# A hybrid encoder layer on one core: another begin, earlier loads and sums, and 26 identity transposes in front of the first real one

## The chip, the core and the metric

The kernel runs on one core of a Trainium2 chip. The core has a matrix engine (PE, or TensorE; its weight loads are listed as PEld), a vector engine (DVE), a scalar engine (ACT), GpSimd (POOL), and SP, which here only issues transfers; 16 DMA engines move data between the chip's memory and the core's own memory (SBUF, and PSUM for the results of PE). The engines work through their own lists of instructions in order and wait for each other by semaphores. The metric is the device time of one execution in microseconds (us), the median of several.

## The reference

One layer of an encoder runs over two requests with the same weights: a sample of 512 tokens and a prompt of 1024, each behind 16 learned meta tokens. All is float32.

```
h = rmsnorm(x, g_mix)
z = h @ w_in                                 # q, k, v, u, gate_na, gate_fn
y_na = neighbourhood_attention(q, k, v, rel_bias, meta_bias) @ w_branch_na
y_fn = fourier_mix(u) @ w_branch_fn          # real part of a 2-D DFT
mixed = sigmoid(gate_na) * y_na + sigmoid(gate_fn) * y_fn
x = x + mixed @ w_out
a = relu(rmsnorm(x, g_mlp) @ w_up)
x = x + (a * a) @ w_down
```

D_MODEL is 1024, there are 8 heads of 64, and the MLP is 4096 wide. At the end stands another rmsnorm, and the meta tokens are dropped. Tokens attend to a neighbourhood of 8 rows by 16 columns of a 64-wide grid and to the meta tokens.

## The kernel before, in words

**Precision.** PE multiplies a rounded form of float32 ("fp32r" in the profile). Each operand is therefore split into a high part (a cast, by ACT, L155 for weights, L136 for results in PSUM) and a low part (the difference, by POOL or DVE, L157 or L137; L159 and L160 do the same with a scale). A product is three matmuls: hi x hi, hi x lo, lo x hi. `mm3` (the matmuls of L132) runs the first two kinds alternately over the 8 blocks of the 1024 rows, then the third. With `late="b"` (new in the diff's call) those that need the low part of the right operand, here the value weights, come last instead of those that need the low part of the left one. 24 matmuls of 128x512 make one block of results.

**The begin.** The sample comes first. `read` loads tokens (tile "xt", three buffers), normalizes them (L178 to L184: squares and root on ACT, reciprocal, refinement and the scaling into "hn" on DVE), and PE transposes 128x128 blocks against the identity (L194) into ps_t, from which "hT" is split. Meta rows come first, then the four tiles of 128 tokens. In between, four pieces of the value weights are loaded and split. `project_v` then multiplies: 24 matmuls for the meta rows and 24 for each tile. Behind that stand the weights of K and Q of the first pair of heads (`qk_weights`), the tables of the mask and biases (`tables`), and the attention, whose first matmuls have the lines L531 to L533.

**The attention of the sample.** For each unit of rows and heads a bias tile "bm" is loaded (L774 to L781), scores go to ps_s (L647, L648), the softmax runs on DVE and ACT (L652 to L656), the weights are transposed (L660) and multiplied with the values (L680). The values went through memory (vd, vf).

**Gates, folding, merge.** `gates` runs 16 steps, each of 24 matmuls, and lets other work advance between them by a list `beside` of generators with a first and a last step. One of these is `fold_u`: it loads a piece of w_in in transposed form and the channel DFT, multiplies them (L259) and stores the result "wu". `merge_na` multiplies attention's result with w_branch_na, whose blocks it loads into the tile "relu" (L825).

**Fourier, merge, projection.** `fourier_channels`, `fourier_positions` (with cosine and sine tables; `sines` loads a sine table from POOL's queue, L1030), `merge_fn`, then `project_out` with the weights "w_raw<-in_w_out" split into "wo_hi" and "wo_lo". It also loads x again into four tiles "acc" for the residual sum (L1091).

**The MLP.** `Up` does the sample's up projection while its generator `reading` normalizes the prompt's tokens beforehand (L184 into "r"). The prompt goes through the same stages, and its MLP is done in class `Halves` as a scheme of combined halves with fewer products: the weights of the down projection are first added up on DVE (L1642), then cast by ACT and split by POOL. The result of each block leaves PSUM by a sum on DVE (L1668), called an eviction below.

**What sets the order.** Each engine's list follows from the order in which the code is written, and a scheduler that brings instructions forward where their data allow. `behind(marks)` holds what is written inside it behind the instructions marked, and `pinned()` holds it behind the latest instruction of every engine. SP issues transfers in order, and a transfer into a tile waits for the tile's earlier users, so one that waits holds up all behind it.

Of the kernel before, what the change touches and what calls it, by code (L numbers as in the profile page):

```python
# [17 lines left out]
F32 = mybir.dt.float32  # L18
# [8 lines left out]
D = 1024  # L27
# [41 lines left out]
class Layer:  # L69
    def __init__(self, tc, ctx, ins, outs):  # L70
# [16 lines left out]
        nc.sync.dma_start(self.sgn, ins["sgn"])  # L87
        self.small = ctx.enter_context(tc.tile_pool(name="small", bufs=4))
        self.wpool = ctx.enter_context(tc.tile_pool(name="w", bufs=2))
        self.wv = {}  # L90
        self.meta_values = None
# [81 lines left out]
    def norm(self, x, gain, out, n=128, junk=None):  # L173
# [10 lines left out]
        nc.vector.scalar_tensor_tensor(out=out, in0=x, scalar=y, in1=gain[:n], op0=ALU.mult, op1=ALU.mult)  # L184
# [16 lines left out]
    def tables(self, marks):  # L201
# [15 lines left out]
        with self.behind(marks):  # L217
            nc.sync.dma_start(mask, self.ins["colmask"])
            nc.sync.dma_start(win, self.ins["rel_win"])
# [78 lines left out]

    def value_weights(self, q, to=None, lo_engine=None, raw="raw"):
        return self.weights(self.ins["w_in"][q * 256:(q + 1) * 256, VC:VC + 512].rearrange("(kt p) c -> p kt c", p=128), to,  # L300
                            lo_engine=lo_engine, raw=raw)

    def qk_weights(self, pr, to=(None, None)):
        return (self.weights(self.rows("w_in", KCOL + pr * 128), to[0], lo_engine=self.nc.vector if pr else None),
                self.weights(self.rows("w_in", QC + pr * 128), to[1], scale=-DH ** -0.5))

    def project_v(self, name, T, hT, p, wv):
# [12 lines left out]
        for t in range(-1 if meta is None else 0, T // 128):  # L320
# [3 lines left out]
            self.mm3(ps[:n, :], [(hT[0][:, kt, pos:pos + n], hT[1][:, kt, pos:pos + n],  # L324
                                  wv[kt // 2][0][:, kt % 2, :], wv[kt // 2][1][:, kt % 2, :]) for kt in range(8)])
            vs = p.tile([128, 512], F32R, name="pt0", tag="pt0", bufs=self.ptb).bitcast(F32)
            nc.vector.tensor_copy(vs[:n], ps[:n])
# [22 lines left out]
    def run(self, order):  # L350
# [6 lines left out]
        for i, (name, T) in enumerate(order):  # L357
# [5 lines left out]
            if i == 0:  # L363
                with pool("first", "right") as p:
                    gain = p.tile([128, D], F32, name="gain")
                    reading = self.read(name, T, hT, lambda: p.tile([128, D], F32, name="xt", bufs=3),
                                        lambda: p.tile([128, D], F32, name="hn", bufs=2), gain)
                    next(reading)
                    next(reading)
                    for q in range(4):  # L370
                        next(reading, None)
                        self.wv[q] = self.value_weights(q, self.pair(p, [128, 2, 512], bufs=4), self.nc.vector, ("raw", "raw", "hi", "lo")[q])
                    marks = self.mark((mybir.EngineType.SP,))
                    w0 = self.qk_weights(0)
# [1496 lines left out]
```

## Time and profile before

| | |
|---|---|
| runs of the kernel, median | 1923.19 us (1922.71 to 1925.18, 3 runs) |
| the profiled execution | 1927.61 us |
| its span | 1925.8 us |
| granted clock over the span | 0.998 |
| busy: PE, PEld | 1892.8 us (98%), 1588.0 us |
| busy: DVE, POOL, ACT | 1117.8 us, 816.5 us, 753.1 us |
| moved by DMA | 358.38 MB, 186 GB/s on average |

A line of the profile gives an instruction's line in the kernel, its engine, its operation and its tiles, written as out<-in with buffer numbers left out. "ps_mm", "ps_s", "ps_t" and "ps_o" are PSUM banks by their tags and are used in turn, so a name does not tell the stage; the time does. In a timeline row the two numbers ahead are start and duration in us; several instructions in a row are joined (x8), and brackets tell how long the engine had stood idle and what ended it. In the chain of work that ended last the numbers are start, length and what. In waits of an engine they are the sum in us, the number of times and the longest. A view by windows gives for each stretch its length, the busy time of each engine with its number of instructions in brackets, and then the clock granted to PE (1.00 is full speed), the busy share of the DMA engines, and GB/s.

### The profile page before, as it was taken

How to read it: one execution, taken by the hardware profiler on the slowest of the kernel's cores; microseconds unless marked ns; L12 is line 12 of the kernel's file. 1: busy time of each engine (PE TensorE's matmuls, PEld its weight loads, DVE VectorE, ACT ScalarE, POOL GpSimd, SP SyncE). 2: the span in 40 equal slices, each digit the busy share in tenths (PEclk: the TensorE clock that was granted, in tenths of full speed). 3: DMA queues.
4: the chain of work that ended last, by engine and by line, in shares of the span. 5: the costliest groups of instructions: out<-in, count | busy, mean ns of one | idle time of the engine just before them, and what ended most of it. 6: DMA issues, size and time to landing. Idle time of an engine off the chain costs nothing.

```text
span 1925.8 us, 26107 instructions
## 1 busy us (share of the span) xinstructions
PE 1892.8 (98%) x9435; PEld 1588.0 (82%) x9435; DVE 1117.8 (58%) x1749; ACT 753.1 (39%) x1351; POOL 816.5 (42%) x674
## 2 busy tenths in 40 slices
PE   7999999999999999999999999999999999999998
PEld 5888888888888888888898878888888888888886
DVE  5771554787625567660427376656665326758856
ACT  3674333443315556541223234333333333333434
POOL 1335543455422233342233218887882323323531
PEclk9999999999999999999999999999999999999999
DMA  6757873687756455463452523444446778567733
GB/s 221 192 152 236 232 218 124 208 271 251 237 191 173 121 145 156 120 233 105 117 158 85 175 99 121 158 173 164 173 155 250 269 250 285 207 218 281 277 118 127
DMA packets 312945, 358.38 MB, mean 186 GB/s; under 512 B 51768, under 2 KB 222392, under 8 KB 312264
## 3 DMA queue, kind: packets, MB, share of 16 engines
q1 hardware_dynamic: 295056, 334.93, 53.0%
q0 software_dynamic: 17760, 21.80, 5.0%
q8 instruction: 74, 1.21, 0.3%
q14 instruction: 55, 0.45, 0.1%
HBM read 263.06 MB, written 96.16 MB: 187 GB/s over the span
## 4 chain that ended last, share of the span: by engine, by line
PE 89%; DMA 4%; DVE 2%; issue 2%; POOL 1%; ACT 1%; SPq 0%; POOLq 0%; DVEq 0%; ACTq 0%
PE ps_mm L132 23%; PE ps_o L132 22%; PE ps_s L132 19%; PE ps_t L132 11%; PE ps_mm L531 3%; PE ps_mm L532 3%; PE ps_mm L533 3%; PE ps_o L680 2%; PE ps_t L660 1%; DMA relu<-in_w_na 1%; DMA bm<-g_un 1%; DMA sin<-in_sin_prompt 1%; PE ps_s L648 1%; PE ps_s L647 1%; PE ps_t L194 0%
## 5 line engine op out<-in xcount | busy, mean ns | idle before, releaser
L157 POOL TENSOR_TENSOR w_lo<-w_raw,w_hi 128x1024 fp32r<-128x1024 f32 x69 | 177.1, 2567 | 217.9 <-ACT w_hi L155 151.9
L157 POOL TENSOR_TENSOR w_lo<-raw,w_hi 128x1024 fp32r<-128x1024 f32 (+1 forms) x49 | 100.0, 2044 | 202.1 <-ACT w_hi L155 196.2
L155 ACT CAST w_hi<-w_raw 128x1024 fp32r<-128x1024 f32 x88 | 92.5, 1051 | 180.1 <-PE ps_s L132 58.5
L157 DVE TENSOR_TENSOR h_lo<-long,h_hi 128x1024 fp32r<-128x1024 f32 x54 | 77.1, 1428 | 94.1 <-ACT h_hi L155 94.1
L531 PE MATMUL ps_mm<-hT,w_hi 128*128 128x512 f32 (+2 forms) x296 | 121.5, 410 | 0.0
L532 PE MATMUL ps_mm<-hT,w_hi 128*128 128x512 f32 (+2 forms) x296 | 110.4, 373 | 0.0
L533 PE MATMUL ps_mm<-hT,w_lo 128*128 128x512 f32 (+2 forms) x296 | 110.4, 373 | 0.0
L155 ACT CAST h_hi<-long 128x1024 fp32r<-128x1024 f32 x54 | 56.7, 1050 | 101.6 <-PE ps_s L132 25.1
L654 ACT ACTIVATE sc<-sc,ast 128x288 f32<-128x288 f32 (+4 forms) x96 | 53.9, 561 | 68.3 <-DVE ast L652 68.0
L155 ACT CAST w_hi<-raw 128x1024 fp32r<-128x1024 f32 (+1 forms) x49 | 40.9, 840 | 100.9 <-DVE raw L1642 54.4
L157 DVE TENSOR_TENSOR hs_lo<-short,hs_hi 128x512 fp32r<-128x512 f32 x54 | 72.3, 1339 | 13.9 <-ACT hs_hi L155 11.7
L1421 POOL TENSOR_TENSOR x<-w_hi,x 128x512 fp32r<-128x512 f32 (+1 forms) x39 | 64.9, 1663 | 18.4 <-ACT x L1418 18.4
L680 PEld LDWEIGHTS ps_o<-pt,vb 104*64 104x64 f32 (+6 forms) x576 | 62.4, 163 | 9.7 <-POOL vb L617 2.6
L132 PE MATMUL ps_t<-gate,x 128*128 128x512 f32 x276 | 66.5, 390 | 0.0
L533 PEld LDWEIGHTS ps_mm<-hT,w_lo 128*128 128x128 f32 x296 | 55.7, 188 | 10.4
L680 PE MATMUL ps_o<-pt,vb 104*64 104x128 f32 (+6 forms) x576 | 62.1, 243 | 1.9 <-POOL vb L617 1.2
L617 POOL TENSOR_TENSOR vb<-vr,vb 96x384 fp32r<-96x384 f32 (+4 forms) x48 | 48.6, 1031 | 34.7 <-ACT vb L616 34.7
L132 PE MATMUL ps_mm<-gate,x 128*128 128x512 f32 x256 | 63.2, 389 | 0.0
L774 POOL MEMSET bm<- 64x96 f32 (+2 forms) x64 | 11.2, 175 | 117.1 <-DVE ast L652 101.7
L132 PEld LDWEIGHTS ps_t<-gate,x 128*128 128x128 f32 x276 | 51.7, 188 | 10.9 <-ACT w_hi L136 0.2
L652 DVE CUSTOM_DVE_ANT_0 sc<-ps_s,bm 128x288 f32<-128x288 f32 (+4 forms) x96 | 46.4, 483 | 23.6 <-issue 10.7
L532 PEld LDWEIGHTS ps_mm<-hT,w_hi 128*128 128x128 f32 x296 | 56.2, 190 | 1.6
(714 smaller groups left out, 5574.4 us busy)
## 6 DMA issues: line engine op xcount, KB each, us to landing
long<-hidden_prompt SPq DMA_DIRECT2D x54, 512.0 KB
w_raw<-in_w_in SPq DMA_DIRECT2D x52, 512.0 KB
raw<-in_w_down SPq DMA_DIRECT2D x39, 512.0 KB
w_raw<-in_w_up SPq DMA_DIRECT2D x34, 512.0 KB
hidden_prompt<-h SPq DMA_DIRECT2D x32, 512.0 KB
short<-hidden_sample SPq DMA_DIRECT2D x54, 256.0 KB
w_lo<-in_w_down SPq DMA_DIRECT2D x18, 512.0 KB
w_raw<-in_w_out SPq DMA_DIRECT2D x16, 512.0 KB
```

Source lines behind the costliest of these rows:

```text
L132: self.nc.tensor.matmul(out, a, b, start=(i == 0 and not more), stop=(i == len(terms) - 1), skip_group_check=more)
L155: nc.scalar.copy(out=hi, in_=raw)
L157: (lo_engine or nc.gpsimd).tensor_tensor(out=lo, in0=raw, in1=hi.bitcast(F32), op=ALU.subtract)
L531: nc.tensor.matmul(ps, a[0], b[0], start=(kt == 0), stop=False)
L532: nc.tensor.matmul(ps, a[0], b[1], start=False, stop=False)
L533: nc.tensor.matmul(ps, a[1], b[0], start=False, stop=(kt == 7))
L617: nc.gpsimd.tensor_tensor(out=lo, in0=vs, in1=hi.bitcast(F32), op=ALU.subtract)
L647: nc.tensor.matmul(ps[:, :W], qs[hh][:, qc], ks[hh][:, 0, kw[0], kw[1]], start=True, stop=False)
L652: nc.vector.tensor_tensor_reduce(out=sc[:, :W], in0=ps[:, :W], in1=bm[:, :W], scale=1.0, scalar=3e38, op0=ALU.add, op1=ALU.min, accum_out= ...
L654: nc.scalar.activation(out=sc[:, :W], in_=sc[:, :W], func=AF.Exp, bias=st[:, 0:1], scale=-1.0, accum_out=st[:, 1:2])
L680: nc.tensor.matmul(po[:m, j * 128:(j + 1) * 128], v, x, start=(i == 0), stop=(i == len(ops) - 1))
L1421: (engine or self.nc.gpsimd).tensor_tensor(out=w[1], in0=raw, in1=w[0].bitcast(F32), op=ALU.subtract)
```

## The change

It joins several edits.

- **Begin.** `read_first` replaces `read` for the sample. It loads x0, gain, w0, x1, w1, meta, w2, w3, x2, x3 in this order; x2 and x3 go into tiles "k" that the attention uses later. PE's list begins with 26 transposes of the identity into a PSUM bank that nothing reads. The first tile's last scaling is done in two halves of columns. Meta rows follow the third tile; their high and low parts are laid side by side in 48 columns, so that 16 matmuls do and a copy and a sum add up the result. The low part of K's weights is made by DVE instead of POOL. The small load "sgn" comes later.
- **Bias.** Six tiles bm are loaded ahead, before the last tile of the values is multiplied.
- **Folding.** `fold_u`'s loads are one step (0) and its matmuls the steps 2 to 9.
- **Residual.** The four loads of x into "acc" are issued behind the Fourier positions, pinned.
- **Reading.** The normalization of the prompt during the sample's `Up` is pinned.
- **Sines.** The second sine table of the prompt is loaded in two pieces of columns.
- **Sums.** In `Halves.down` the sums of weights for a coming step are given out between the evictions of the current one.

```diff
@@ norm
+        for i in range(parts):
+            cs = slice(i * D // parts, (i + 1) * D // parts)
+            nc.vector.scalar_tensor_tensor(out=out[:, cs], in0=x[:, cs], scalar=y, in1=gain[:n, cs], op0=ALU.mult, op1=ALU.mult)
@@ the new reading of the sample
+    def read_first(self, name, T, hT, gain, p, more):
+        nc = self.nc
+        xs, hns, raws = {}, {}, {}
+        def load(t):
+            n = NM if t < 0 else 128
+            xs[t] = p.tile([128, D], F32, name="xt", bufs=3) if t < 2 else more()
+            nc.sync.dma_start(xs[t][:n], self.ins["meta_tokens"] if t < 0 else self.ins[f"x_{name}"][t * 128:(t + 1) * 128, :])
+        def load_w(q):
+            raws[q] = self.wtile(("raw", "raw", "hi", "lo")[q], [128, 2, 512]).bitcast(F32)
+            nc.sync.dma_start(raws[q], self.value_rows(q))
+        def norm(t):
+            n = NM if t < 0 else 128
+            hns[t] = p.tile([128, D], F32, name="hn", bufs=2)
+            self.norm(xs[t][:n], gain, hns[t][:n], n, parts=1 if t else 2)
+        def turn(t):
+            self.transpose_in(hns[t], hT, 0 if t < 0 else self.lead + t * 128, NM if t < 0 else 128)
+        def split(q):
+            self.wv[q] = self.split_sb(raws[q], *self.pair(p, [128, 2, 512], bufs=4), lo_engine=nc.vector)
+        load(0)
+        self.gain(gain, "g_mix")
+        warm = self.psum("o")
+        for _ in range(26):
+            nc.tensor.transpose(warm[:, :128], self.ident, self.ident)
+        load_w(0)
+        load(1)
+        load_w(1)
+        load(-1)
+        load_w(2)
+        load_w(3)
+        for t in range(2, T // 128):
+            load(t)
+        norm(0)
+        split(0)
+        turn(0)
+        with self.behind(self.mark((mybir.EngineType.Activation, mybir.EngineType.DVE))):
+            norm(1)
+            split(1)
+            split(2)
+        turn(1)
+        split(3)
+        with self.behind(self.mark((mybir.EngineType.Activation, mybir.EngineType.DVE))):
+            norm(2)
+            turn(2)
+            for t in (-1, 3):
+                norm(t)
+                turn(t)
@@
+    def qk_weights(self, pr, to=(None, None), late=()):
+        return (self.weights(self.rows("w_in", KCOL + pr * 128), to[0], lo_engine=self.nc.vector if pr or late else None, lo_marks=late),
                 self.weights(self.rows("w_in", QC + pr * 128), to[1], scale=-DH ** -0.5))
@@ project_v
-        for t in range(-1 if meta is None else 0, T // 128):
+        order = list(range(T // 128))
+        for t in order if meta is not None else order[:-1] + [-1] + order[-1:]:
+            if meta is None and t == T // 128 - 1:
+                with self.behind(self.mark((mybir.EngineType.SP,))):
+                    self.first_bias(p, T)
             n = NM if t < 0 else 128
             pos = 0 if t < 0 else self.lead + t * 128
             ps = self.psum()
-            self.mm3(ps[:n, :], [(hT[0][:, kt, pos:pos + n], hT[1][:, kt, pos:pos + n],
-                                  wv[kt // 2][0][:, kt % 2, :], wv[kt // 2][1][:, kt % 2, :]) for kt in range(8)])
+            if t < 0:
+                own = p.tile([128, 512], F32R, name="pt1", tag="pt1", bufs=self.ptb)[:, :8 * 48].rearrange("p (k c) -> p k c", k=8)
+                nc.gpsimd.tensor_copy(own[:, :, NM:2 * NM].rearrange("p k (g c) -> p k g c", c=8),
+                                      self.zero[:, None, None, 0:8].to_broadcast([128, 8, 2, 8]))
+                for i in range(2):
+                    nc.scalar.copy(out=own[:, :, 32 * i:32 * i + NM], in_=hT[i][:, :, 0:NM].bitcast(F32))
+                for i in range(2):
+                    for kt in range(8):
+                        nc.tensor.matmul(ps[:48], own[:, kt], wv[kt // 2][i][:, kt % 2, :], start=(kt + i == 0), stop=(kt + i == 8))
+            else:
+                self.mm3(ps[:n, :], [(hT[0][:, kt, pos:pos + n], hT[1][:, kt, pos:pos + n],
+                                      wv[kt // 2][0][:, kt % 2, :], wv[kt // 2][1][:, kt % 2, :]) for kt in range(8)],
+                         late="b" if meta is None and t < 2 else "a")
             vs = p.tile([128, 512], F32R, name="pt0", tag="pt0", bufs=self.ptb).bitcast(F32)
-            nc.vector.tensor_copy(vs[:n], ps[:n])
+            if t < 0:
+                low = p.tile([128, 512], F32R, name="pt1", tag="pt1", bufs=self.ptb).bitcast(F32)[:n]
+                nc.scalar.copy(out=low, in_=ps[32:32 + n])
+                nc.vector.tensor_tensor(out=vs[:n], in0=ps[:n], in1=low, op=ALU.add)
+            else:
+                nc.vector.tensor_copy(vs[:n], ps[:n])
@@ run, the sample's begin
                     gain = p.tile([128, D], F32, name="gain")
-                    reading = self.read(name, T, hT, lambda: p.tile([128, D], F32, name="xt", bufs=3),
-                                        lambda: p.tile([128, D], F32, name="hn", bufs=2), gain)
-                    next(reading)
-                    next(reading)
-                    for q in range(4):
-                        next(reading, None)
-                        self.wv[q] = self.value_weights(q, self.pair(p, [128, 2, 512], bufs=4), self.nc.vector, ("raw", "raw", "hi", "lo")[q])
+                    self.read_first(name, T, hT, gain, p, lambda: att.tile(
+                        [128, 2, T // 64 + 2, 64], F32R, name="k", tag="k", bufs=4).rearrange("p i a b -> p (i a b)").bitcast(F32)[:, :D])
                     marks = self.mark((mybir.EngineType.SP,))
-                    w0 = self.qk_weights(0)
+                    w0 = self.qk_weights(0, late=self.mark((mybir.EngineType.DVE,)))
 
                     rest = self.tables(marks)
-                    for _ in reading:
-                        pass
                     self.project_v(name, T, hT, att, self.wv)
@@ fold_u among the gates
-                beside = [(self.fold_u(mp.tile([128, 512], F32, name="relu", bufs=2)[:, :128],
+                beside = [self.fold_u(mp.tile([128, 512], F32, name="relu", bufs=2)[:, :128],
                                        [t.bitcast(F32) for _ in range(2) for t in flat(self.pair(mp, [128, 2, 512]))],
-                                       lambda: flat(self.pair(fn, [128, 4, 128], bufs=4))), 0, 9),
-                          (fold, 5, 13)]
+                                       lambda: flat(self.pair(fn, [128, 4, 128], bufs=4)))]
+                beside = [(*beside, 0, 1), (*beside, 2, 10), (fold, 5, 13)]
@@ behind the Fourier positions
+                if small:
+                    acc = [ap.tile([128, D], F32, name=f"acc{t}") for t in range(T // 128)]
+                    for t in range(T // 128):
+                        nc.sync.dma_start(acc[t], self.ins[f"x_{name}"][t * 128:(t + 1) * 128, :])
...
-            acc = [ap.tile([128, D], F32, name=f"acc{t}") for t in range(T // 128)]
@@ the first bias tiles
+    def first_bias(self, p, T):
+        blocks = row_blocks(T // 64)
+        wide = max(b["n"] * w for b in blocks for w in KW)
+        for u in range(6):
+            h, R, j = u // (4 * len(blocks)), u // 4 % len(blocks), u % 4
+            self.bms.append(p.tile([128, wide], F32, name="bm", bufs=6))
+            self.bias(self.bms[-1], h, j, KW[j], blocks[R])
 
@@
+            if self.bms:
+                bm = self.bms.pop(0)
+            else:
+                bm = p.tile([128, wide], F32, name="bm", bufs=6 if T == 512 else 4)
+                with self.behind(spread if h == 0 else []):
+                    self.bias(bm, h, j, w, b)
@@ sines
-        self.nc.gpsimd.dma_start(t, self.ins[f"sin{i}_{name}"].rearrange("(t p) k -> p t k", p=128))
+        src = self.ins[f"sin{i}_{name}"].rearrange("(t p) k -> p t k", p=128)
+        for ks in (slice(0, 262), slice(262, R + 1)) if i and R > 512 else (slice(0, R + 1),):
+            self.nc.gpsimd.dma_start(t[:, :, ks], src[:, :, ks])
@@ project_out
-        for t in range(nt):
-            nc.sync.dma_start(acc[t], x[t * 128:(t + 1) * 128, :])
@@ Up
-                    next(reading, None)
+                    with layer.pinned():
+                        next(reading, None)
@@ Halves.down
         def load(i):
+            for _ in load_parts(i):
+                pass
+        def load_parts(i):
             if i >= len(steps):
                 return
             rs, rl, rw, *rest = (x.bitcast(F32) for x in self.raws.pop(i))
             n, u = steps[i]
             for x, (_, sign) in zip(rest, self.parts(self.DOWN[n][1], u)[1:]):
                 nc.vector.tensor_tensor(out=rw, in0=rw, in1=x, op=ALU.add if sign > 0 else ALU.subtract)
+                yield
@@
+            loading, sums = iter(()), 0
+            if u == nu - 1 and i + 2 < len(steps):
+                loading = load_parts(i + 2)
+                sums = len(self.parts(self.DOWN[n + 1][1], 1)) - 1
             for t in range(nh):
                 product(banks[t], t, n, [u])
                 if u == nu - 1:
                     evict(n, t)
+                    if t < sums:
+                        with layer.pinned():
+                            next(loading, None)
             with layer.pinned():
                 if u == nu - 1:
-                    load(i + 2)
+                    for _ in loading:
+                        pass
```

Three places show how lists change; the instruction at a place is given by line, operation and tiles. The first is ACT's list in the begin, where L155 is a cast of weights (from "w_hi" and "w_lo" the third and fourth piece of the value weights, the "w_raw" behind them K's), L159 is the scaling of Q's, "hT" a cast of transposes and "hn,st" the squares of a tile. Before:

```order
L155 CAST w_hi<-w_hi 128x1024
L179 ACTIVATE st<-st,zero 128x1
L155 CAST w_hi<-w_lo 128x1024
L155 CAST w_hi<-w_raw 128x1024
L136 CAST hT_95<-ps_t 128x4x128 x2
L159 ACTIVATE w_hi<-w_raw 128x1024
L136 CAST hT_95<-ps_t 128x4x128 x2
```

With the change:

```order
L155 CAST w_hi<-w_hi 128x1024
L155 CAST w_hi<-w_lo 128x1024
L178 ACTIVATE hn,st<-k 128x1024
L179 ACTIVATE st<-st,zero 128x1
L155 CAST w_hi<-w_raw 128x1024
L159 ACTIVATE w_hi<-w_raw 128x1024
L136 CAST hT_94<-ps_t 128x4x128 x2
L178 ACTIVATE hn,st<-xt 16x1024
```

Before, the casts of the third and the fourth tile's transposes stood on either side of Q's scaling; now K's cast and Q's scaling stand in front of those of the second, behind the squares of x2 (tile "k").

The second place is SP's list around the loads of "acc". Before, two and two of them stood among the loads of w_branch_na ("relu"):

```order
L825 DMA relu<-in_w_na 128x4x128 x6
L1091 DMA acc_3347<-in_x_sample 128x1024
L1091 DMA acc_3348<-in_x_sample 128x1024
L825 DMA relu<-in_w_na 128x4x128
L1091 DMA acc_3349<-in_x_sample 128x1024
L1091 DMA acc_3350<-in_x_sample 128x1024
L825 DMA relu<-in_w_na 128x4x128
L866 DMA raw<-in_w_fnA 128x4x128
```

With the change they stand between the last loads of the Fourier merge and the first of w_out:

```order
L956 DMA gain<-in_w_fnB 128x4x128
L535 DMA acc_3177<-in_x_sample 128x1024
L535 DMA acc_3178<-in_x_sample 128x1024
L950 DMA wfn_3171<-raw 128x512
L950 DMA wfn_3175<-raw 128x512
L535 DMA acc_3179<-in_x_sample 128x1024
L535 DMA acc_3180<-in_x_sample 128x1024
L149 DMA w_raw<-in_w_out 128x2x512 x2
```

The loads of w_branch_na now follow each other, and w_out's first load comes behind all four of "acc".

In the prompt's down projection, DVE's list had six evictions (L1668) in a row and then the sums of weights (L1642):

```order
L1668 TENSOR_TENSOR u_13636<-u_13630,ps_mm 128x512
L1668 TENSOR_TENSOR u_13637<-u_13631,ps_mm 128x512
L1642 TENSOR_TENSOR raw<-raw 128x1024
L157 TENSOR_TENSOR hs_lo<-short,hs_hi 128x512
L1642 TENSOR_TENSOR raw<-raw,w_hi 128x1024
L157 TENSOR_TENSOR h_lo<-long,h_hi 128x1024
L1642 TENSOR_TENSOR raw<-raw,w_hi 128x1024
L1642 TENSOR_TENSOR w_lo<-w_lo 128x1024
```

With the change (the lines are L1764 and L1737):

```order
L1764 TENSOR_TENSOR u_13659<-u_13653,ps_t 128x512
L1737 TENSOR_TENSOR raw<-raw 128x1024
L1764 TENSOR_TENSOR u_13660<-u_13654,ps_t 128x512
L1737 TENSOR_TENSOR raw<-raw,w_hi 128x1024
L1764 TENSOR_TENSOR u_13661<-u_13655,ps_o 128x512
L1737 TENSOR_TENSOR raw<-raw,w_hi 128x1024
L1764 TENSOR_TENSOR u_13662<-u_13656,ps_o 128x512
L1764 TENSOR_TENSOR u_13663<-u_13657,ps_mm 128x512
```

Three sums moved from behind the sixth eviction to between the first four.

More of the change, by code (lines that the diff above doesn't have):

```diff
@@ L86, in __init__ @@
         self.sgn = edge.tile([128, 2], F32, name="sgn")
-        nc.sync.dma_start(self.sgn, ins["sgn"])
         self.small = ctx.enter_context(tc.tile_pool(name="small", bufs=4))
@@ L90, in __init__ @@
         self.wv = {}
+        self.bms = []
         self.meta_values = None
@@ L171, in gain, with norm @@
         return g
-    def norm(self, x, gain, out, n=128, junk=None):
+    def norm(self, x, gain, out, n=128, junk=None, parts=1):
         nc = self.nc
@@ L183, in norm @@
         nc.vector.scalar_tensor_tensor(out=y, in0=a, scalar=1.5, in1=y, op0=ALU.add, op1=ALU.mult)
-        nc.vector.scalar_tensor_tensor(out=out, in0=x, scalar=y, in1=gain[:n], op0=ALU.mult, op1=ALU.mult)
+        for i in range(parts):
+            cs = slice(i * D // parts, (i + 1) * D // parts)
+            nc.vector.scalar_tensor_tensor(out=out[:, cs], in0=x[:, cs], scalar=y, in1=gain[:n, cs], op0=ALU.mult, op1=ALU.mult)
     def transpose_in(self, hn, hT, pos, n=128):
@@ L217, in tables @@
         with self.behind(marks):
+            nc.sync.dma_start(self.sgn, self.ins["sgn"])
             nc.sync.dma_start(mask, self.ins["colmask"])
@@ L299, in value_weights, with value_rows @@
+    def value_rows(self, q):
+        return self.ins["w_in"][q * 256:(q + 1) * 256, VC:VC + 512].rearrange("(kt p) c -> p kt c", p=128)
     def value_weights(self, q, to=None, lo_engine=None, raw="raw"):
[L300 to L304, printed above, removed]
+        return self.weights(self.value_rows(q), to, lo_engine=lo_engine, raw=raw)
@@ L485, in run @@
                 rest = list(wout)
-            self.project_out(hp_, mp, self.ins[f"x_{name}"], T, h2T, rest, acc, mlp, marks)
+            self.project_out(hp_, mp, T, h2T, rest, acc, mlp, marks)
             out.close()
@@ L639, in unit @@
             qs, ks = state[pr]
-            bm = p.tile([128, wide], F32, name="bm", bufs=6 if T == 512 else 4)
-            with self.behind(spread if h == 0 else []):
-                self.bias(bm, h, j, w, b)
+            if self.bms:
[4 more added lines that the diff above has]
+                    self.bias(bm, h, j, w, b)
             ps = self.psum("s")
@@ L1082, in out_weights, with project_out @@
             yield self.weights(src, place and (place() if callable(place) else self.pair(*place)), lo_engine=self.nc.vector if i == 2 else None)
-    def project_out(self, hp, p, x, T, m, wo, acc, mlp, marks):
+    def project_out(self, hp, p, T, m, wo, acc, mlp, marks):
         nc = self.nc
```

## The prediction

> **What bounds the kernel now.** I read the page's busy times first, then the chain that ended last in order of time, and then, place by place, the waits of TensorE (PE).
>
> ```profile
> PE 1892.8 (98%) x9435; PEld 1588.0 (82%) x9435; DVE 1117.8 (58%) x1749; ACT 753.1 (39%) x1351; POOL 816.5 (42%) x674
> PE 89%; DMA 4%; DVE 2%; issue 2%; POOL 1%; ACT 1%; SPq 0%; POOLq 0%; DVEq 0%; ACTq 0%
> ```
>
> PE is busy for 98% of the span of 1925.8 us, and 89% of the chain is PE itself. The other 11% of the chain are steps of other engines and transfers, during most of which PE still worked, or its share of busy time couldn't be 98%. So a change here can win only where PE stands still or runs at a lower clock. A warm group shows the pace:
>
> ```profile
> 312.93 5.44 PE ps_o L132 x24
> ```
>
> 24 matmuls of 128x512 in 5.44 us are 0.227 us each. Whatever a row costs beyond this is a loss. These rows of the chain hold the places where PE lost a microsecond or more and that the change touches (start, length, what):
>
> ```profile
> 2.13 5.87 DMA xt<-in_x_sample
> 22.05 3.25 DVE w_lo L157
> ...
> 51.55 5.71 DMA vf_sample<-vd_sample
> 57.66 7.19 DMA bm<-g_un
> ...
> 153.52 6.00 DMA w_hi<-in_w_uT
> ...
> 236.84 9.68 DMA relu<-in_w_na
> 247.29 4.20 PE ps_s L132 x12
> ...
> 989.81 10.99 DMA sin<-in_sin_prompt
> ```
>
> And PE's own waits there, each from the waits of its stretch:
>
> ```profile
> PE ps_mm L132 <- DVE w_lo L157: 1.8, 1, 1.8
> ...
> PE ps_t L660 <- DVE sc L656: 2.1, 4, 1.0
> ...
> PE ps_mm L259 <- DMA w_hi<-in_w_uT: 1.0, 1, 1.0
> ...
> PE ps_s L132 <- ACT hid_hi L155: 2.1, 1, 2.1
> ...
> PE ps_t L194 <- DVE gate L137: 0.9, 1, 0.9
> ...
> PE ps_o L132 <- DMA sin<-in_sin_prompt: 1.0, 1, 1.0
> ...
> PE ps_t L132 <- POOL w_lo L157: 1.2, 1, 1.2
> ```
>
> Six of these seven lie behind the begin. They sum to 1.0 + 1.0 + 2.1 + 0.9 + 1.0 + 1.2 = 7.2 us, and a start-to-start count of the matmuls adds 0.1 to 0.2 to each for the refilled pipeline. All else in the kernel keeps its order on PE, so the forecast is a sum over these places and the begin.
>
> **The begin.** What PE does, and then what ACT and DVE do for it:
>
> ```profile
> 8.06 1.00 PE L194 MATMUL ps_t<-ident,hn 16*128 16x16 f32 x8 [8.06 <-DVE hn L184]
> 11.69 1.94 PE L194 MATMUL ps_t<-ident,hn 128*128 128x128 f32 x8 [2.62 <-DVE st L181]
> ...
> 22.22 1.04 PE L194 MATMUL ps_t<-ident,hn 128*128 128x128 f32 x8
> ...
> 47.47 0.29 PE L531 MATMUL ps_o<-hT,w_hi 128*128 128x272 f32 x1
> ```
>
> ```profile
> 22.86 1.07 ACT L136 CAST hT<-ps_t 128x512 fp32r<-128x512 f32 x2 [1.13 <-PE ps_t L194]
> 23.82 1.07 ACT L159 ACTIVATE w_hi<-w_raw 128x1024 fp32r<-128x1024 f32 x1
> ...
> 25.52 1.28 DVE L137 TENSOR_TENSOR hT<-ps_t,hT 128x512 fp32r<-128x512 f32 x2
> 26.72 1.28 DVE L184 SCALAR_TENSOR_TENSOR hn<-xt,st,gain 128x1024 f32<-128x1024 f32 x1
> ```
>
> Eight transposes take 1.94 us at 11.69 and 1.04 at 22.22: the first ran at half the clock. The attention's first matmul (L531) starts near 47.2. Between 8.06 and there PE needs 4 x 24 x 0.227 = 21.8 us for the four tiles, 24 x 0.227 = 5.4 for the meta rows and about 4 for transposes, 31 together, and took 39: it lost some 8. The change removes 8 matmuls of the meta rows (16 of 48 columns instead of 24), 8 x 0.227 = 1.8 us. It takes POOL's w_lo away from beside DVE, where the row at 22.05 shows a DVE difference at 3.25 us. Against it stands the data. DMA was nearly full in these stretches (from the left: PE, PEld, DVE, ACT and POOL busy; the last three columns: clock, DMA share, GB/s):
>
> ```profile
> 6.83:10.24 3.41, 1.00 (x8) 0.93 (x8) 2.04 (x7) 2.22 (x6) 0.00 (x0) 1.00 0.97 366
> 10.24:13.65 3.41, 1.96 (x9) 1.90 (x10) 3.29 (x7) 2.19 (x5) 0.00 (x0) 1.00 0.87 287
> ```
>
> The new order puts x2 and x3 (no longer waiting for a buffer) ahead of the K and Q weights, and ACT now casts K and scales Q before it casts the second tile's transposes. Before, the scaling of Q (23.82) stood behind two casts of transposes. The same bytes lie ahead of Q as before; the queue starts it earlier by the 1.4 us between the first issue and x0's at 2.13, and by the room that shares of 0.87 left. So I estimate Q at 20.4 to 21.7, its scaling done at 21.5 to 22.8 (1.07), the second tile's two casts at 22.6 to 23.9, and, since DVE then still has one normalization (1.28, as at 26.72) and two differences (1.28 together, as at 25.52) in its order, the second tile's matmuls flowing from 24 to 26. Behind them PE needs three tiles less what is done, meta 16 x 0.227 and three sets of transposes, about 21.3 us: L531 at 45.3 to 47.3. The 26 identity transposes end near 1.8 + 26 x 0.24 = 8 at half clock, which is when the first real tile is wanted (x0 now lands first, 2.13 + 5.87 less 1.4 or more; gain is next), so they cost nothing; scaling in halves saves up to 0.64 ahead of the first transpose, and the first tile then waits for weights anyway. PE may go cold in the gap ahead of the second tile, and what that costs a row further down shows: 1.9 us. I take **0** for the begin, with bounds -3 and +3.
>
> The Trainium skill, TensorE: Matmul & The Clock Gate, Part 4 (PE-mode transpose), says that a transpose does not count as PE activity for the clock; by it the 26 would warm nothing. The trace speaks against it here: full clock was there by 16.7 us, after a stretch in which mostly transposes had run. By the rule the sum would be up to 2 us worse, since the first tile's 24 matmuls would run cold where weights don't hold them; by the trace it stays as it is.
>
> **First bias tiles.** Six bm tiles are loaded while the values are computed, and not behind vf (51.55 + 5.71) as at 57.66, where the tile needed 7.19. The four waits on L656 sum to 2.1; the chain puts the bm load ahead of the 1.0 only, the small ones ahead are partly its echo. **-1.2**, from -0.5 to -1.8. DVE is next in line there: the sc chain of each unit then sets the pace.
>
> **Folding of u.** The loads go out as a step of their own, two steps of the gates (about 6.35 us each: 166.29 to 172.64 in the next fence) before their matmuls. The load of 153.52 took 6.00 and PE waited 1.0 for it; 12.7 us cover it twice over. **-1.2** (0 at worst, if the first gate steps lack their data instead).
>
> ```profile
> 166.29 5.46 PE ps_o L132 x24
> 172.64 5.46 PE ps_mm L132 x24
> ```
>
> **The residual loads.** This is the largest term. SP issued four 512-KB loads of x between the loads of the merge's weights:
>
> ```profile
> 229.22 1.55 SPq L1091 DMA_DIRECT2D acc<-in_x_sample  x2
> ...
> 233.43 1.39 SPq L1091 DMA_DIRECT2D acc<-in_x_sample  x2
> ```
>
> The relu load of 236.84 took 9.68 by the chain. The view of that tile, which has a landing only for some of its loads, gives a median of 3.9:
>
> ```profile
> DMA to landing us min/median/max: 2.4/3.9/5.4
> ```
>
> Without 2 MB ahead it lands some 5 us sooner, and PE needs it 2.1 sooner. The wait has an echo, since the clock fell:
>
> ```profile
> 245.40:248.80 3.40, 1.51 (x7) 1.25 (x8) 0.55 (x1) 0.62 (x1) 1.29 (x1) 1.00 1.01 292
> 248.80:252.30 3.50, 3.50 (x12) 2.92 (x11) 0.77 (x3) 0.00 (x0) 0.58 (x1) 0.51 0.21 48
> ```
>
> A window with PE busy for 1.51 of 3.40 us is followed by one with a clock of 0.51. 3.5 us at 0.51 hold the work of 1.8. So 2.1 + 0.2 + 1.8 = 4.1, rounded to **-4.0**; 0 if the load stays late for another reason. The 2 MB now go out ahead of the output projection's weights, whose loads were already tight:
>
> ```profile
> 272.04 0.53 SPq L149 DMA_DIRECT2D w_raw<-in_w_out  x1
> ...
> 281.03 17.66 SPq L149 DMA_DIRECT2D w_raw<-in_w_out  x4
> ...
> 297.07 1.22 DVE L157 TENSOR_TENSOR wo_lo<-w_raw,wo_hi 128x1024 fp32r<-128x1024 f32 x1
> ```
>
> PE waited about 0.35 for the wo_lo at 297.07. The first issue goes from 272 to some 279, behind two of the four loads; a 512-KB load in a full queue takes about 1.4 (512 KB at 366 GB/s). The last weights come 0 to 2 us late: **+0.8**.
>
> **Reading the prompt, sin, sums.** The norm of the next stage's tile now runs later, pinned inside the MLP, so DVE's gate no longer waits behind it at 351: 0.9 plus 0.3 in the pipeline and at 342, **-1.3** (0 if another DVE piece takes the place). The sin tile is loaded in two halves of columns; PE wanted the first at 999.5 and the second 3 us later, and the whole landed at 989.81 + 10.99 = 1000.8: **-1.2** (0 if a half lands no sooner). In the tail DVE adds up weights (1.22 each) between its evictions:
>
> ```profile
> 1721.22 0.69 DVE L1668 TENSOR_TENSOR u<-u,ps_mm 128x512 f32<-128x512 f32 x1 [0.67 <-PE ps_mm L132]
> 1721.83 1.22 DVE L1642 TENSOR_TENSOR raw<-raw 128x1024 f32<-128x1024 f32 x1
> ```
>
> An eviction of 0.69 every 1.36 us leaves 0.67 idle; a sum of 1.22 in it delays the next eviction by at most 0.55, which two PSUM banks per name cover. Three of the sums move in front of the row at 1721.22, the cast and POOL's difference come some 3 us sooner, and the wait of 1.2 at L132 goes: **-1.4** (0 to -1.4).
>
> **Sum.** 0 - 1.2 - 1.2 - 4.0 + 0.8 - 1.3 - 1.2 - 1.4 = -9.5 us. The profiled execution took 1927.61 us (span 1925.8 and 1.8 around it), so it would take 1918.1; it lies 4.4 above the median of the runs, 1923.19, and 1923.19 - 9.5 = **1913.7 us** is the forecast, with its own range from 1910 to 1917.5 by the uncertainty of the terms (3 us on the begin, 1 to 2 on the rest).
>
> **Rivals.** First, *the begin loses*: ACT, in order, holds the second tile until Q has come, PE stands idle from about 19 to 25, the clock falls as at 248.8, and L531 comes at about 50: +3; the stalls behind give back a little (the bias tiles' 1.2 had slack from an early begin). For it: ACT's order; against it: the rows that put Q at 23.8 before were throttled by buffers. -9.5 + 3 + 1 = -5.5, 1917.7. Second, *the stalls move*: relu's load stays late, since other transfers fill the queue (share 1.01 in the window from 245.4), and only 1 us of the 4.1 comes; with sin or the sums failing too, -9.5 + 3.1 + 1.2 = -5.2, 1918. Third, *the begin wins*: Q lands by 19 and the second tile flows from 21.5, L531 at 43.5: -12.5 to -13, 1910.5. Fourth, on the other side, *the projection starves*: 2 MB at 1.4 us per 512 KB are 5.6 us in front of w_out, PE has nothing else there, and the wait draws a cold window of 1.8, 7.4 in all; if the w_up loads, which stand behind w_out on SP (17.66 us of issue), are late by as much again, 14.8: -10.3 + 14.8 = +4.5, 1927.7. It decides for slower from a delay of 12 us on. Against it: only two of the four loads precede the first w_out, and the projection has its first blocks by 292. Fifth, *it does nothing measurable*: removed waits are re-formed on DVE, which is busy for 58%; that would be 1921.
>
> **Chances.** Forecast 0.58; the begin loses 0.13; the stalls move 0.12; the begin wins 0.08; nothing measurable 0.06; starving 0.03. A difference under 0.2% (3.8 us) cannot be told from no change, so faster is under 1919.3: all of the forecast and of the third, most of the first two, 0.85 in all; same 0.11; slower 0.04. The range is **1908.5 to 1920**.
>
> **What would show it.** The begin: L531's first matmul at 45 to 47.5; the second tile's hT casts directly behind Q's scaling; clock at full by the first tile. The terms: no wait of PE on L259 near 160, on hid_hi at 247 with no window at half clock behind it, on gate at 351, on sin at 1000, on POOL's w_lo at 1730; a wait of under 2 us on wo_lo near 298. The forecast is wrong if L531 comes after 49, if a new wait of over 3 us stands before the projection, or if the evictions of the tail hold PE.

## The result and the profile after

The changed kernel takes 1944.08 us (median of 4, 1942.3 to 1945.07) beside 1922.95 for the kernel before on the same chip: a ratio of 1.0107, interval 1.0092 to 1.0122. It is 21 us slower; the forecast was 1913.7, within 1908.5 to 1920. Two of the runs below each had one execution with a granted clock of only 0.67 or 0.75 (2628.77 and 2358.09 us), which their numbers leave out.

The profiled execution has a span of 1940.5 us. The first lines of its page, busy times and the chain:

```profile
PE 1899.9 (98%) x9453; PEld 1594.8 (82%) x9453; DVE 1105.9 (57%) x1751; ACT 755.3 (39%) x1354; POOL 811.2 (42%) x675
PE 91%; DVE 3%; issue 2%; DMA 2%; ACT 2%; POOL 0%; SPq 0%; POOLq 0%; ACTq 0%; DVEq 0%
```

They tell nothing: PE is still busy for 98%. A matmul at half the clock counts as busy for longer (eight transposes further down take 1.94 us instead of 1.04), which hides a part of the loss. What tells is PE's waits by stretch. At the places of the forecast nothing is left at the folding, the merge's weights, the gates, the sines and the sums; one new line stands at 360 to 500 us, in the sample's MLP:

```profile
PE ps_t L196 <- DVE r L186: 20.8, 8, 6.1
```

PE's eight groups of transposes of the prompt's tokens (L196), one for each tile of 128, wait for the scaling of the tile (L186), 20.8 us in all. In the profile before, the groups of instructions of the same stretch have no wait at PE's transposes; of before and then of the change:

```profile
L194 PE MATMUL ps_t<-ident,r 128*128 128x128 f32 x64 | 8.3, 272 | 0.0
```

```profile
L196 PE MATMUL ps_t<-ident,r 128*128 128x128 f32 x64 | 9.6, 299 | 20.8 <-DVE r L186 20.8
```

Their mean length also grows from 272 to 299 ns: some run at half the clock. Windows of the changed kernel around the first wait show the same (the third number from the right is the clock):

```profile
372.00:376.00 4.00, 1.21 (x6) 0.67 (x4) 0.27 (x2) 1.78 (x4) 0.00 (x0) 1.00 0.93 303
376.00:380.00 4.00, 0.70 (x4) 0.73 (x5) 3.15 (x8) 1.08 (x2) 0.00 (x0) 0.56 1.13 361
380.00:384.00 4.00, 4.00 (x15) 3.39 (x14) 1.39 (x2) 1.76 (x3) 0.49 (x1) 0.58 1.02 344
```

By a start-to-start count of the matmuls, 360 to 500 us lost 27.6 us: 22.1 in the eight waits and 5.5 in slow matmuls. The chain shows what stands ahead of the first one:

```profile
368.89 5.25 DMA r<-in_x_prompt
374.22 1.15 ACT r L178 x2
...
377.88 1.29 DVE r L186
379.17 0.14 issue
379.30 1.94 PE ps_t L196 x8
```

The tile is only requested at 368.89, and its load, squares, root and scaling, 10.3 us, lie in a row in front of PE. The chain goes through the load in the same way for the third and the fifth tile: 6.1, 2.6 and 3.4 us of wait, 12.1 of the 20.8. For the seventh, 2.6 us, it names a step of DVE that ended just then. For the second, fourth, sixth and eighth, 1.5 to 1.6 us each, it doesn't pass through the load at all. There the squares stand in ACT's list behind a cast of weights (L155) that waits for PE, and a step of DVE of 2.2 us stands in front of the scaling. The fourth tile:

```profile
413.09 3.64 PE ps_mm L132 x16
...
416.80 0.04 ACT w_hi L155
...
417.76 1.14 ACT r L178 x2
...
419.42 2.24 DVE hid_lo L1254
...
422.96 1.29 DVE r L186
```

In the timelines of the kernel before, the load of the first tile is issued at 340.37, that tile is scaled by 350.1, and PE turns it at 378.94:

```profile
340.37 0.33 SPq L288 DMA_DIRECT2D r<-in_x_prompt  x1
```

```profile
348.85 1.28 DVE L184 SCALAR_TENSOR_TENSOR r<-r,st,r 128x1024 f32<-128x1024 f32 x1
...
400.39 1.28 DVE L184 SCALAR_TENSOR_TENSOR r<-r,st,r 128x1024 f32<-128x1024 f32 x1
```

```profile
378.94 1.04 PE L194 MATMUL ps_t<-ident,r 128*128 128x128 f32 x8
...
402.50 1.03 PE L194 MATMUL ps_t<-ident,r 128*128 128x128 f32 x8
```

The first tile had 28.8 us to spare. The third, scaled by 401.67 and turned at 402.50, had 0.8, and from there on the timelines show 1.6 to 4.6. From the third tile on, none could be moved back by the length of a load (5.25 us above) without PE waiting.

### The profile page after: what moved, and what is told of

Same layout as the page of the kernel before. It is cut to its first block, busy times and chain, and to the rows that moved or that the text cites. A ratio compares the mean times of both kernels' runs of the same rounds, so it can differ in the third digit from the quotient of the medians.

```text
span 1940.5 us, 26170 instructions
## 1 busy us (share of the span) xinstructions
PE 1899.9 (98%) x9453; PEld 1594.8 (82%) x9453; DVE 1105.9 (57%) x1751; ACT 755.3 (39%) x1354; POOL 811.2 (42%) x675
## 4 chain that ended last, share of the span: by engine, by line
PE 91%; DVE 3%; issue 2%; DMA 2%; ACT 2%; POOL 0%; SPq 0%; POOLq 0%; ACTq 0%; DVEq 0%
PE ps_o L132 23%; PE ps_mm L132 23%; PE ps_s L132 19%; PE ps_t L132 11%; PE ps_mm L618 3%; PE ps_mm L619 3%; PE ps_mm L620 3%; PE ps_o L770 2%; PE ps_t L750 1%; DMA r<-in_x_prompt 1%; PE ps_t L196 1%; DMA w_raw<-in_w_in 1%; PE ps_s L737 1%; PE ps_s L738 1%; DVE r L186 1%
## 5 line engine op out<-in xcount | busy, mean ns | idle before, releaser
L157 POOL TENSOR_TENSOR w_lo<-w_raw,w_hi 128x1024 fp32r<-128x1024 f32 x68 | 171.3, 2520 | 245.4 <-ACT w_hi L155 135.9
L155 ACT CAST w_hi<-w_raw 128x1024 fp32r<-128x1024 f32 x88 | 92.3, 1049 | 180.7 <-PE ps_s L132 53.0
L155 ACT CAST h_hi<-long 128x1024 fp32r<-128x1024 f32 x54 | 56.8, 1052 | 136.1 <-PE ps_o L132 28.0
L157 DVE TENSOR_TENSOR hs_lo<-short,hs_hi 128x512 fp32r<-128x512 f32 x54 | 63.2, 1171 | 17.5 <-ACT hs_hi L155 17.5
L155 ACT CAST w_hi<-raw 128x1024 fp32r<-128x1024 f32 (+1 forms) x49 | 41.1, 840 | 67.4 <-PE ps_mm L132 15.3
L620 PEld LDWEIGHTS ps_mm<-hT,w_lo 128*128 128x128 f32 x296 | 55.7, 188 | 10.3
L742 DVE CUSTOM_DVE_ANT_0 sc<-ps_s,bm 128x288 f32<-128x288 f32 (+4 forms) x96 | 46.3, 482 | 21.1 <-issue 10.3
```

Source lines behind the costliest of these rows:

```text
L155: nc.scalar.copy(out=hi, in_=raw)
L157: (lo_engine or nc.gpsimd).tensor_tensor(out=lo, in0=raw, in1=hi.bitcast(F32), op=ALU.subtract)
L620: nc.tensor.matmul(ps, a[1], b[0], start=False, stop=(kt == 7))
L742: nc.vector.tensor_tensor_reduce(out=sc[:, :W], in0=ps[:, :W], in1=bm[:, :W], scale=1.0, scalar=3e38, op0=ALU.add, op1=ALU.min, accum_out= ...
```

## The experiments

**Which edit.** One edit of the change is undone:

```diff
                 if g:
-                    with layer.pinned():
-                        next(reading, None)
+                    next(reading, None)
```

> All of the change but one edit: the reading of the prompt during the sample's MLP is not pinned. Theory A (the pin holds each load of a prompt tile until the engines have finished a group, and the transfer of 5.25 to 6.43 us and the norm behind it then stand in front of PE's transposes): the eight waits of PE on L186 between 372 and 482 us, 22.1 us by the start-to-start count, and the slow matmuls behind them, 5.5 us, go: 1944.1 - 27.6 = 1916.5, within 1914 to 1919. Rival B (DVE and the queues are too full there with the sums of L1265 and the loads of w_down, pin or no pin): over 1930.

1915.01 us (1914.68 to 1915.45), 0.9948 of the kernel before (1924.12 in these runs), interval 0.9933 to 0.9963. The eight waits are gone. The single edit costs 29 us, and the rest of the change gains 9.1.

The other way round, the kernel before with this edit alone:

> The kernel before, with one edit: the reading is pinned. Theory A: the pin costs by itself what it costs in the change, 27.6 us less about 1 for the wait on gate that it removes: 1924 + 26 = 1950, within 1945 to 1954. Rival E (the pin only hurts together with another edit, such as the residual loads that now stand later on SP): under 1935.

1950.92 us, a ratio of 1.0135 (1.0121 to 1.0149): +27. The profile has the same line:

```profile
PE ps_t L194 <- DVE r L184: 19.7, 8, 3.6
```

The pin needs no other edit; rival E falls.

**Which part of the edit.** A step of the reading loads a tile, transposes the one before it and normalizes the new one. Three kernels hold only one of the three behind the group (each by the same marks, taken at the start of the step):

```diff
+            marks = self.mark(self.lanes + (mybir.EngineType.PE,)) if self.read_pin else []
+            pin = lambda part: self.behind(marks if part in self.read_pin else [])
-            nc.sync.dma_start(xt[:n], ...)
+            with pin("load"):
+                nc.sync.dma_start(xt[:n], ...)
...
+                with pin("turn"):
+                    self.transpose_in(*last)
...
+            with pin("norm"):
+                self.norm(xt[:n], gain, hn[:n], n)
```

> As the change, but of each step of the reading only the load of x is held behind the group; norm and transposes are free. Theory A: as slow as the change, 1940 to 1946. Rival C (what costs is that ACT and DVE may not begin the norm earlier): near 1917.

> As the change, but only the norm is held; load and transposes are free. Theory A: x is there 5 us earlier than in the change, so at most the first wait of 6.3 us is partly left: 1916 to 1922. Rival C: 1940 or more.

> As the change, but only the transposes are held; load and norm are free. Theory A: as without a pin, 1914 to 1919. Rival D (the place of the transposes on PE, two or three rows later than without a pin, is what costs): over 1930.

Load alone: 1944.04 us (three executions), ratio 1.0105 (1.0084 to 1.0125), as slow as the whole pin. Norm alone: 1916.18, 0.9956 (0.9941 to 0.9971). Transposes alone: 1915.03, 0.9948 (0.9933 to 0.9963). The waits of PE in 360 to 500 us, with the load held and then with the norm held:

```profile
PE ps_t L197 <- DVE r L187: 21.9, 8, 6.4
```

```profile
PE ps_t L197 <- DVE r L187: 0.7, 1, 0.7
```

It is the held load that costs. Rivals C and D fall: with x there early, a norm that starts behind the group is in time for all tiles but the first, by 0.7 us. With the load held, the norm is late for every tile although nothing holds it: for the first, third, fifth and seventh ACT stands idle for the transfer, and for the others its squares again come behind the cast that PE releases. So holding the load alone is enough to change the lists of the other engines too.

**Giving the load its time back.** All stays pinned, but each step loads the next step's tile into a second buffer:

```diff
-            xt = xts()
-            nc.sync.dma_start(xt[:n], ...)
+            xt = xs[t]
+            if t + 1 < T // 128:
+                load(t + 1)
```

> The change with the reading still pinned whole, but each step loads the tile of the next step into a second buffer, so that a transfer has one group of about 11 us more. Theory A: the transfer of 5.25 to 6.43 us leaves the path, the norm stays there: most waits on the scaling go, 1916 to 1922. Rival C (the norm's own chain on ACT and DVE is what is late): 1930 or more.

1925.04 us, ratio 1.0002 (0.9993 to 1.0011): neither as theory A expected nor as rival C.

```profile
PE ps_t L196 <- DVE r L186: 8.0, 2, 6.1
```

Two waits are left of eight: the first tile has no step ahead of it, and its load is issued together with the second's (369.91 and 371.12). With a half-clock window behind them they lose 10.0 us by the start-to-start count. So the first tile's load was also set free, one group earlier:

```diff
         load(0)
         self.gain(gain, "g_mix")
+        yield
...
                 if g:
                     with layer.pinned():
                         next(reading, None)
+                else:
+                    next(reading, None)
```

> As the run with loads one step ahead (all steps pinned), and the first tile's load before all pins, one group earlier. In that run only the first two tiles made PE wait (6.3 and 2.0 us, and the half clock behind them, 10.0 us in all between 360 and 400 us), since the first had no step ahead of it. Theory A: these go too, 1915.0 to 1917.5, although norms and transposes are still pinned. Rival C (the norms are late by themselves): 1921 or more.

1915.85 us, ratio 0.9954 (0.9938 to 0.9971). PE waits for 1.9 us in two pieces. The pin costs little when the load has one group of lead; what made the change slow is that the load was issued too late, which put the transfer, or the norm that waits for it, in front of PE.

**The other edits.** The kernel before with folding, residual loads, sines and sums only, begin and bias tiles and reading as before:

> The kernel before with four of the edits: folding in two steps, residual loads behind the Fourier positions, sines in halves, sums between evictions; begin, bias tiles and reading as before. By the terms of the forecast: -1.2 - 4.0 + 0.8 - 1.2 - 1.4 = -7.0, so 1917. If the begin and the bias tiles gave more than forecast (the attention begins at 44.1 to 45.6 instead of 47.2), they are the rest to 1915.0: no_begin at 1918 to 1919 would say so.

1919.99 us, ratio 0.9979 (0.9970 to 0.9988), measured against 1923.86: -3.9 where the terms gave -7.0, so slower than either expectation. One part of the missing 3 us is a new wait at 267 us, for a result of the Fourier channels (tile "us"). Neither the kernel before nor the change has it (the run with 8 identity transposes has 0.5), and its cause wasn't tried:

```profile
PE ps_s L132 <- DVE us L137: 0.7, 1, 0.7
```

Another part is found with the run without the pin, and with the residual loads back in their old place:

> As without the pin, and the four residual loads back in their old place among the loads of w_branch_na. By the forecast's term (-4.0, and +0.8 at the projection): 1915.0 + 3.2 = 1918.2. Theory H (the execution profiled before the change had a longer wait there than is usual, and the half-clock window behind it, since in the run of the pin alone the same wait was 1.1 us with no such window): 1915.0 + 1.1 - 0.8 to 1915.0 + 1.2, so 1915.3 to 1916.2.

1916.46 us, ratio 0.9963 (0.9950 to 0.9977). Against 1915.01 of the run without the pin, which was timed in another set of runs, that is 1.5; by the ratios it is 0.0015 of 1924, 2.9; and against the two kernels with 4 and 8 identity transposes below, which were timed beside it and have the new place, it is 0.9 to 1.0. The intervals overlap, so the runs put the term at some 1 to 3 us and not clear of noise: below the forecast's 3.2, and a little above the range of theory H. The profile speaks more plainly. PE waits there for 0.9 us, after 0.3 at 236 us, no window of half clock follows, and the load that came last took 8.88 us:

```profile
PE ps_s L132 <- ACT hid_hi L155: 0.9, 1, 0.9
```

```profile
236.00:242.00 6.00, 4.82 (x21) 3.43 (x20) 1.38 (x2) 1.14 (x2) 3.16 (x3) 1.00 1.14 361
242.00:246.00 4.00, 4.00 (x30) 3.76 (x29) 2.43 (x11) 0.00 (x0) 0.58 (x1) 1.00 0.33 86
```

The run of the pin alone, whose code up to there is that of the kernel before, has the same 0.9. And it has no wait for the sines. Its transfers around the sine load (issued at 1014.62), and those of the profile before (issued at 989.81), in 40 slices of GB/s each over the 12 us from 1014 and from 989:

```profile
GB/s 0 0 0 0 137 382 178 212 321 389 367 361 404 369 411 396 348 313 383 397 404 347 77 42 14 14 7 14 0 0 0 0 0 0 0 0 0 0 0 0
```

```profile
GB/s 0 0 0 0 0 191 82 314 348 396 403 236 209 230 237 223 278 299 292 292 278 251 334 279 236 160 139 153 125 56 35 42 28 28 21 28 21 14 0 0
```

The same bytes moved more slowly in the profile before (mostly 200 to 300 GB/s and not 310 to 410), and there the last packets trailed at under 60 GB/s for nine slices of 0.3 us and ended 10.6 us after the issue, in the other execution for five and 7.8 us after it.

**The identity transposes.** Without the pin, with none, 4 or 8 instead of 26:

```diff
-        for _ in range(26):
+        for _ in range(0):      # 4 and 8 in the other two
```

> As without the pin, and with no identity transposes in front. Theory F (they only warm the clock ahead of a stretch that waits for weights and for ACT): within 1 us of 1915.0, the first real transposes at half clock (1.9 us for eight, and not 1.23). Theory G (they are worth the clock of the first tile): the first tile takes up to 3 us longer and all comes 1.5 to 3 us later, 1916.5 to 1918.

> As without the pin, with 4 identity transposes in place of 26. In the lists the transfer of vf stands ahead of the weights' load again (with none it stood behind one that waits for a buffer, and PE waited 5.8 us for the values). Theory F (what the run with none lost was this place in SP's list, and not the clock): 1913.5 to 1915.5, the attention beginning at 43 to 44.5. Theory G (the clock of the first tile): 1917 to 1921.

> As without the pin, with 8 identity transposes; the lists of SP and POOL are those of 26, and ACT casts one piece later (Q's scaling now behind the second tile's casts). Theory F: 1913.5 to 1915.5. Theory G: 1916 to 1920.

With none 1921.61 us (0.9987, 0.9978 to 0.9997), with 4 it is 1915.43 (0.9957, 0.9945 to 0.9969), with 8 1915.60 (0.9958, 0.9946 to 0.9971). None is 6 us slower, more than either theory expected, but not for the clock of the first tile. Its attention begins at 43.12, earlier than in any other run:

```profile
43.12 0.29 PE L618 MATMUL ps_o<-hT,w_hi 128*128 128x272 f32 x1
```

What it loses, it loses later, on values that aren't there (PE's waits at 50 to 75 us, then SP's timeline):

```profile
PE ps_o L770 <- POOL vb L704: 5.7, 1, 5.7
```

```profile
53.01 0.38 SPq L149 DMA_DIRECT2D w_raw<-in_w_in  x1
53.48 2.97 SPq L855 DMA_DIRECT2D vf_sample<-vd_sample  x4
```

With other lengths ahead the scheduler wrote another order: a load of weights, which waits for a buffer until 53.01, now stands ahead of the values' transfer (L855), which had been issued at 50.12 without it. With 4 and 8 the transfer is ahead again, and the time is that of 26. So the total goes as theory F has it: 26 identity transposes buy nothing here that 4 don't, and what made none slow was, by its wait of 5.7 us, the order of SP's list. What the clock of the first tile is worth by itself isn't shown, since ACT's list differs with the count too.

## Why the prediction was wrong

**The step that failed** is "Reading the prompt", where the forecast put -1.3 "(0 if another DVE piece takes the place)". It priced what the pin took away from 351 us and not what it moved. The moved step issues a load of 512 KB, and the forecast didn't ask when its result is wanted. The rows were there: load at 340.37 and 389.47, scaling at 348.85 and 400.39, transposes at 378.94 and 402.50. So the third tile's load was issued 13.0 us before its transposes and had 0.8 us of slack; in the change it was issued 9.3 us before PE was free for them. In place of -1.3 the step cost +27.6 by the trace, and 29 in the runs (1944.1 - 1915.0): the eight waits, 22.1, and the slow matmuls behind them, 5.5. No rival named this place; the one on the slower side named w_out, which made no wait at all. It was argued away there with "only two of the four loads precede the first w_out", which SP's list of the change contradicts: all four do, and PE still didn't wait.

**Its gain didn't come either.** Once the reading is free, PE's wait on gate is back at 340 us with 0.9; only the pin removes it.

**The rest of the sum** was -9.5 + 1.3 = -8.2 and was measured at -9.1 (1915.01 against 1924.12), but by errors that cancel.

- Begin: 0 was forecast, with L531 at 45.3 to 47.3. It starts at 45.56 in the change and at 44.08 without the pin, against 47.47: -1.9 to -3.4. Begin and bias tiles together are the difference of the runs with and without them, -9.1 + 3.9 = -5.2. The faster begin goes past the bound of -3. The sign "clock at full by the first tile" held for that tile's transposes alone: in the change a part of its matmuls ran at 0.54 (last section). ACT does hold the second tile until Q is scaled, as the forecast said, but Q arrived by 19.08 and not at 20.4 to 21.7, so the estimate of the queue was 1.3 late or more (ACT's timeline of the change):

```profile
17.47 1.05 ACT L155 CAST w_hi<-w_raw 128x1024 fp32r<-128x1024 f32 x1 [1.09 <-DMA w_raw<-in_w_in]
19.08 1.06 ACT L159 ACTIVATE w_hi<-w_raw 128x1024 fp32r<-128x1024 f32 x1 [0.57 <-DMA w_raw<-in_w_in]
20.05 1.05 ACT L136 CAST hT<-ps_t 128x512 fp32r<-128x512 f32 x2
```

- Bias: -1.2 forecast; the waits on the scores' scaling fall from 2.1 to 1.2 in the change and 0.8 without the pin. Right in kind, about 1.
- Folding and sums: the waits of 1.0 and 1.2 are gone, as forecast.
- Residual loads: -4.0 forecast. The wait is gone, but two other executions with the loads in the old place had it at 0.9 and no half-clock window, so the larger part of 2.1 + 1.8 belonged to the one execution that was profiled. The runs with this edit undone put it at 1 to 3, not clear of noise.
- Sines: -1.2 forecast. The one other trace with the old order has no wait there, so probably nearly 0, for the same reason.
- The projection: +0.8 forecast; PE doesn't wait there at all, and the first load of w_out is issued at 270.44, not at some 279.

That the profiled execution lay 4.4 us above the median was said in the forecast, and was then treated as if it were spread evenly. By the traces a part of it sat in two of the terms, the residual loads and the sines.

Four smaller slips changed little. The six waits behind the begin sum to 8.3 by the rows shown; 7.2 counts L660 with its longest wait alone. 3.5 us at a clock of 0.51 lose 1.7 us, and not 1.8. The fourth rival's 12 us of delay leave +1.7, less than the 3.8 that the forecast itself asked for. And the 26 identity transposes ended at 6.1 to 7.4 us, not at 8.

## What to carry to other kernels

Ask of everything that a pin moves when its result is wanted, transfers first: the slack is the time between the end of the work and its use, row by row, for the tightest tile and not only the first. When the profiled execution is slower than the median, the largest stalls in it are the first suspects, and a second execution of the same order tells which are usual. A pin behind the work of a group was cheap here once the load was issued a group ahead. And holding one transfer can reorder the lists of other engines, so the waits that appear need not all lie behind the transfer itself.

## What the runs showed of the hardware

Identity transposes alone raised the clock. PE had done nothing else, and 26 of them took 4.42 us in the change and 5.81 in the run with only the norm held:

```profile
1.63 4.42 PE L333 MATMUL ps_o<-ident 128*128 128x128 f32 x26 [1.63 <-POOL ident masks.py:199]
```

```profile
1.62 5.81 PE L339 MATMUL ps_o<-ident 128*128 128x128 f32 x26 [1.62 <-POOL ident masks.py:199]
```

Four of them took 1.12 us and eight 1.97 in the runs with fewer, so each further one takes 0.21, and 26 at that pace would be 5.8. The second row is this slow pace to its end; in the first, by the starts in the trace, the step from one to the next fell from 0.21 to 0.11 us at the fourteenth. The first eight real transposes then took 1.23 us behind 26 (the change) and 1.94 behind none (behind 4 and 8 they took 1.94 too):

```profile
7.62 1.23 PE L196 MATMUL ps_t<-ident,hn 128*128 128x128 f32 x8 [1.58 <-DVE hn L186]
```

```profile
7.89 1.94 PE L196 MATMUL ps_t<-ident,hn 128*128 128x128 f32 x8 [7.89 <-DVE hn L186]
```

The clock column of the windows doesn't show this: it reads 1.00 from 1.6 to 8 us of the change, where half of the 26 ran at the slow pace. The Trainium skill, TensorE: Matmul & The Clock Gate, Part 4 (PE-mode transpose), has it that transposes don't count as activity; these rows speak against that for the float32 transposes here, though the profile doesn't say whether they use the mode that the page means.

The higher clock didn't last. In the change, PE was busy for 1.99 of the 3.5 us from 8.0, and a stretch at half clock followed (without the pin it was 2.07, and none followed):

```profile
8.00:11.50 3.50, 1.99 (x10) 1.16 (x9) 2.62 (x5) 3.50 (x6) 0.00 (x0) 0.97 1.03 370
11.50:15.00 3.50, 3.50 (x10) 2.37 (x9) 2.81 (x5) 2.79 (x5) 0.00 (x0) 0.54 1.05 420
```

And the same begin ran in two ways. Eight profiled executions have the same order up to the attention. In four it started at 45.4 to 45.6 us, and a stretch at half clock fell on the second tile, as in the change (0.51 from 21.5 to 25); in the other four it started at 44.1 to 44.3 without one there, as without the pin. What decides between the two wasn't tried; it moves the start of the attention by some 1.3 us, and so may be a part of the spread of the runs.
